# Long convolutions of a hybrid encoder layer: the filters' spectra as one stream of pieces through DRAM, and the second stage on unsplit spectra

## The chip, the cores and the metric

The kernel runs on one core of a Trainium2 chip. A core has five engines that run side by side, each in its own program order: TensorE (PE, matrix products and transposes, with weight loads shown as PEld), VectorE (DVE), ScalarE (ACT), GpSimd (POOL) and SyncE (SP), and 16 DMA engines that serve queues filled by SP, ACT and POOL. They wait for each other through semaphores. The metric is the device time of one execution in microseconds (us); lower is better.

## What is computed

One layer of a bidirectional encoder on 2048 tokens of 1024 channels, in float32. One projection feeds two token mixers, a gated long convolution (Hyena) and an RWKV-7 scan; their outputs are gated, merged and projected, and a SwiGLU feed-forward network follows, each with a layer norm. The change lies in the Hyena branch:

```python
def hyena_filters(L, fw1, ..., fw4, sin_freq):
    ...                                        # a small MLP of the positions, with sines
    h = (h @ fw4).reshape(L, HY_ORDER, 2, HY_WIDTH)
    window = jnp.exp(-t * deltas[None, :])
    return h * window[:, None, None, :]

def long_conv(z, h_fwd, h_bwd, d_skip):        # FFT of length 2L
    zf = jnp.fft.rfft(z, n=n, axis=1)
    hf = jnp.fft.rfft(h_fwd, n=n, axis=0) + jnp.conj(jnp.fft.rfft(h_bwd, n=n, axis=0))
    y = jnp.fft.irfft(zf * hf[None], n=n, axis=1)[:, :L]
    return y + z * d_skip

def hyena_mixer(u, ...):
    v, x1, x2 = jnp.split(short_conv3(u, conv_w, conv_b), 3, axis=-1)
    z = x1 * long_conv(v, h[:, 0, 0], h[:, 0, 1], sk[0])
    z = x2 * long_conv(z, h[:, 1, 0], h[:, 1, 1], sk[1])
    return z
```

There are 512 channels, so 8 filter spectra of 128 channels: 4 channel blocks c by 2 orders o.

## The kernel before

The kernel first projects (with the RWKV preparation woven in), then runs the RWKV scan (`chain`) beside the rest of the projection, then the long convolutions (`hyena`), then merges, and ends with the feed-forward network. On PE the order in `chain` and `hyena` is written out by hand; on the other engines a scheduler orders instructions by priority and readiness. Inside a hand-written order, side work is a generator, and `pull(gen, need)` takes pieces from it until their stated costs reach `need`.

A transform of length 4096 is done in two stages, 128 times 32. For one channel block:

- `fwd` multiplies z with the first-stage matrices (`Fz`, L1220); ACT copies the result to a tile U (L1222), laid out as 128 partitions (4 groups of 32) by 32 by 128 channels.
- `flip` (L1182 to 1188) swaps the two indices of 32 with four DVE transposes (L1187) per tile, each on 32 channels, into a tile V (three buffers).
- `step3` (L1235) multiplies V, four of its 32 slices at a time (q from 0 to 7), with the second-stage matrix `Mc`. For a filter (`load`, L1244) it does so in four f32 matmuls of 128 columns (L1241), and the result H and a copy with the 32-row groups exchanged, Hs, go to ring tiles; the exchange is four DMAs on SP's queue (L1251). For z (`parts`, L1225) each group from q = 1 on is split first into a rounded part and a rest, by a cast on ACT and a subtraction on DVE, and three 128x512 matmuls (L202, 203 and 204, through `mm3`) follow.
- `product` (L1254) runs over q: it loads H for q + 2, transforms z, multiplies by H and by Hs on DVE (A and B, L1278 and L1279), pulls pieces of filter work, and transforms back (L1263, L1264) into a tile Q, which is flipped as well. `inverse` (L1288) is the last stage (L1293); for the first order DVE multiplies the result with x1 into z (L1355), which goes through `fwd` again.

A filter is made by the generator `filt(c, o)` (L1145): for each q, ACT writes the window (four exponentials, L1166), PE multiplies the MLP's output with fw4 (L1167), DVE multiplies the two (L1171), one piece; then `spec` multiplies with the first-stage matrix (L1157), and ACT copies into a tile U (L1158), another piece. After 16 pieces the tile is flipped by `flip`, that is on DVE, and kept in `Vfs`. Both kinds of piece use eight PE instructions. Each filter is a generator of its own: (0, 0) begins in the last two steps of the scan and ends in the prelude of `hyena`, where it is pulled dry; (c, 1) is pulled in the first product of block c and after it, and (c + 1, 0) in the second product of block c.

The blocks c = 0 to 3 follow each other in `hyena` (L1338): transform of filter (c, 0), end of the block before (`finish`: inverse, copies L1310 on ACT, transposes L1302, products with x2), first product, inverse and forward again, the next block's z, second product, the next block's forward.

Scratch for this stage is a ring of 14 tiles (`ring`, L619; `next`, L1096) and tiles `cu` for the rows that the short convolutions (`short`, L1118) fetch from DRAM.

Of the kernel before, what the change touches and what calls it, by code (L numbers as in the profile page):

```python
# [16 lines left out]
P = 128  # L17
# [5 lines left out]
HT = 4  # L23
# [166 lines left out]
class Layer:  # L190
# [38 lines left out]
    def build(self):  # L229
        tc, nc = self.tc, self.nc  # L230
        with tc.tile_pool(name="dr", bufs=1, space=DRAM) as dr, tc.tile_pool(name="keep", bufs=1, reuse_waits="tile") as keep:
# [8 lines left out]
            self.Yd = T("Yd", [NCH, P, 256])  # L240
            self.Nd, self.Wd = T("Nd", [2, P, 1024]), T("Wd", [2, P, 1024])
# [377 lines left out]
    def ring(self, k, n=512):  # L619
        return self.cm.tile([P, 514], F32, name="rg", tag=f"rg{k % 14}")[:, 0:n]  # L620

    def chain(self):
# [3 lines left out]
        with tc.tile_pool(name="ch", bufs=1, reuse_waits="tile") as s, tc.tile_pool(name="chp", bufs=1, space=PSUM, reuse_waits="tile") as ps:  # L626
# [369 lines left out]
            with tc.manual_schedule(engines={mybir.EngineType.PE}):  # L996
# [18 lines left out]
                for n in range(N):  # L1015
# [5 lines left out]
                    if n == LAST + 1:  # L1021
                        taps = self.filt(0, 0)
# [43 lines left out]
    def open(self):  # L1066
# [3 lines left out]
        cu = self.wp.tile([P, 1024], F32, name="cu0", tag="wraw", bufs=2)  # L1070
# [3 lines left out]
        self.turns = dict(cu=0, row=0, w=0, g=0, A=0, B=0, H=0, Hs=0)  # L1074
        self.smalls, self.Vfs = {}, {}
# [20 lines left out]
    def next(self, name):  # L1096
        first, n = dict(w=(8, 2), g=(10, 2), A=(12, 2), B=(0, 2), H=(2, 3), Hs=(5, 3))[name]
# [47 lines left out]
    def filt(self, c, o):  # L1145
        nc = self.nc
        mm = nc.tensor.matmul
        fw4, delta, skip = self.smalls.pop((c, o))
        if (c, o) != (HT - 1, 1):
            self.small(c + o, 1 - o)  # L1150
        U = self.pre(c)

        def spec(q, g):
            ps, tag, bufs = self.fps
            p = ps.tile([P, 4, P], F32, name="pf", tag=tag, bufs=bufs)
            for j in range(4):
                mm(p[:, j], self.Fc[:, 4 * q + j], g[:, j], start=True, stop=True)  # L1157
            nc.scalar.copy(U[:, 4 * q:4 * q + 4], p)  # L1158

        for q in range(8):  # L1160
            win, g = self.next("w"), self.next("g")
            ps, tag, bufs = self.fps
            p = ps.tile([P, 4, P], F32, name="pg", tag=tag, bufs=bufs)
            for j in range(4):
                n = 4 * q + j
                nc.scalar.activation(win[:, j], delta, AF.Exp, scale=self.tcol[:, n:n + 1])  # L1166
                mm(p[:, j], self.H3[:, n], fw4, start=True, stop=n != 0)  # L1167
                if n == 0:
                    mm(p[:, j], self.e0[0:1], skip[0:1], start=False, stop=True)
            with self.tc.high_priority(offset=2 * FIRST):  # L1170
                nc.vector.tensor_tensor(out=g, in0=p, in1=win, op=ALU.mult)  # L1171
# [19 lines left out]
    def hyena(self):  # L1191
# [3 lines left out]
        with tc.tile_pool(name="hy", bufs=1, reuse_waits="tile") as s, tc.tile_pool(name="hyp", bufs=2, space=PSUM, reuse_waits="tile") as ps:  # L1195
# [29 lines left out]
            def parts(V, q, room):  # L1225
                v = V[:, 4 * q:4 * q + 4]
                if q == 0:
                    return v, None
# [452 lines left out]
```

## Time and profile before

| | us |
|---|---|
| median of 3 runs | 4077.75 |
| lowest and highest run | 4075.48 and 4081.51 |
| profiled execution | 4068.93 |
| its span in the profile | 4067.2 |

A profile has one execution. Its page gives the busy time of each engine; other views of the same trace give busy time by stretches of the span, the waits of an engine (who waited, for what, total time, times, longest), groups of instructions by line and tile, the DMA issues, and a timeline in which a bracket holds the idle time before an instruction and what released it. Times in the views are from the span's start. Names such as L1187 are lines of the kernel before; `V<-U` is output and input tile. The stage of the long convolutions is from about 1668 to 2212 us.

### The profile page before, as it was taken

To read this page: it belongs to the slowest core of one execution; us is meant where nothing else is said; L and a number is where in the kernel's file an instruction comes from. 1 tells how busy PE (TensorE), PEld (TensorE's weight loads), DVE (VectorE), ACT (ScalarE), POOL (GpSimd) and SP (SyncE) were. 2 spreads that over 40 slices of the span, in tenths; PEclk is the share of its full clock that TensorE was granted. 3 is DMA by queue.
4 is the path that set the end of the run, shared out by engine and by line. 5 is a ranking of instruction groups with operands and counts; after the bars stand their busy time and mean duration, and the time that the engine had idled before them with its cause. 6 is when DMAs were issued, how large, how long until landed. Compare 5 with 4: busy or idle time off the path is not lost. (4 is left out here: it accounts for less than half of the span.)

```text
span 4067.2 us, 64483 instructions
## 1 busy us (share of the span) xinstructions
PE 3870.1 (95%) x25872; PEld 3130.6 (77%) x25872; DVE 2421.1 (60%) x3823; ACT 1484.1 (36%) x2912; POOL 76.8 (2%) x107
## 2 busy tenths in 40 slices
PE   8999999899998999888898999999999999999998
PEld 6766557677776777788887899788888878888887
DVE  5456885556656666778877656544444465444444
ACT  3345662223335556756554323211111141111113
POOL 0000000000000000000000000000000000000000
PEclk9999999899898999899999999999999999999999
DMA  4556877666666766412224433411111133111111
GB/s 137 175 168 176 224 205 236 192 195 184 201 205 193 205 198 192 118 50 70 63 74 135 159 114 123 160 58 52 47 47 47 47 104 104 47 47 47 47 47 42
DMA packets 389186, 501.83 MB, mean 123 GB/s; under 512 B 134852, under 2 KB 270541, under 8 KB 388181
## 3 DMA queue, kind: packets, MB, share of 16 engines
q1 hardware_dynamic: 362775, 443.13, 36.3%
q10 hardware_dynamic: 20736, 37.80, 3.1%
q0 software_dynamic: 5376, 16.78, 1.5%
q8 instruction: 204, 3.34, 0.3%
q14 instruction: 95, 0.78, 0.1%
HBM read 352.74 MB, written 127.93 MB: 118 GB/s over the span
## 5 line engine op out<-in xcount | busy, mean ns | idle before, releaser
L202 PE MATMUL acc<-xh,wh 128*128 128x512 f32 x1376 | 606.4, 441 | 9.1 <-ACT xh L197 9.1
L203 PE MATMUL acc<-xl,wh 128*128 128x512 f32 x1376 | 551.9, 401 | 6.4 <-DVE xl L198 6.4
L204 PE MATMUL acc<-xh,wl 128*128 128x512 f32 x1376 | 551.0, 400 | 0.5 <-DVE wl L198 0.5
L1618 DVE TENSOR_TENSOR acc<-pd,acc 128x1024 f32<-128x1024 f32 x320 | 387.7, 1221 | 69.9 <-PE pd L204 64.2
L197 ACT CAST fwh<-raw 128x1024 fp32r<-128x1024 f32 x132 | 138.6, 1050 | 704.7 <-PE pg L203 487.9
L202 PEld LDWEIGHTS acc<-xh,wh 128*128 128x128 f32 x1376 | 262.3, 191 | 127.4 <-issue 46.9
L1646 DVE TENSOR_TENSOR h<-pu,sg 128x512 f32<-128x512 f32 x88 | 60.9, 692 | 493.1 <-PE pu L204 485.7
L204 PEld LDWEIGHTS acc<-xh,wl 128*128 128x128 f32 x1376 | 262.8, 191 | 63.9 <-DVE wl L198 1.0
L203 PEld LDWEIGHTS acc<-xl,wh 128*128 128x128 f32 x1376 | 264.5, 192 | 57.4 <-DVE xl L198 10.2
L198 DVE TENSOR_TENSOR wl<-wraw,wh 128x512 fp32r<-128x512 f32 (+1 forms) x217 | 170.3, 792 | 188.4 <-ACT wh L197 181.2
L202 PE MATMUL pd<-fwh,hh 128*128 128x512 f32 x704 | 276.1, 392 | 2.3 <-DVE acc L1616 1.9
L204 PE MATMUL pu<-fxh,fwl 128*128 128x512 f32 x704 | 277.8, 395 | 0.0
L204 PE MATMUL pg<-fxh,fwl 128*128 128x512 f32 x704 | 277.8, 395 | 0.0
L202 PE MATMUL pg<-fxh,fwh 128*128 128x512 f32 x704 | 276.7, 393 | 0.2 <-DVE fxl L1533 0.2
L203 PE MATMUL pg<-fxl,fwh 128*128 128x512 f32 x704 | 276.8, 393 | 0.0
L203 PE MATMUL pu<-fxl,fwh 128*128 128x512 f32 x704 | 276.4, 393 | 0.0
L202 PE MATMUL pu<-fxh,fwh 128*128 128x512 f32 x704 | 275.9, 392 | 0.4 <-ACT fxh L1532 0.4
L203 PE MATMUL pd<-fwl,hh 128*128 128x512 f32 x704 | 275.6, 391 | 0.0
L204 PE MATMUL pd<-fwh,hl 128*128 128x512 f32 x704 | 274.6, 390 | 0.0
L198 DVE TENSOR_TENSOR fwl<-raw,fwh 128x1024 fp32r<-128x1024 f32 x132 | 161.3, 1222 | 166.6 <-ACT fwh L197 162.6
L197 ACT CAST wh<-wraw 128x512 fp32r<-128x512 f32 (+1 forms) x217 | 151.1, 705 | 198.3 <-PE acc L203 182.0
L1187 DVE STREAM_TRANSPOSE V<-U 128x1024 f32<-128x1024 f32 x96 | 181.1, 1955 | 34.3 <-ACT U L1222 14.1
(299 smaller groups left out, 7617.1 us busy)
## 6 DMA issues: line engine op xcount, KB each, us to landing
wraw<-in_w_in SPq DMA_DIRECT2D x130, 512.0 KB
ABp<-ABd SPq DMA_DIRECT2D x64, 512.0 KB
raw<-in_fg SPq DMA_DIRECT2D x44, 512.0 KB
raw<-in_fu SPq DMA_DIRECT2D x44, 512.0 KB
raw<-in_fd SPq DMA_DIRECT2D x44, 512.0 KB
ud<-ev ACTq DMA_DIRECT2D x84, 256.0 KB
ABd<-AB SPq DMA_DIRECT2D x32, 512.0 KB
gated<-ev SPq DMA_DIRECT2D x64, 256.0 KB
```

Of the source, the lines that this page charges most:

```text
L197: nc.scalar.copy(hi, src)
L198: nc.vector.tensor_tensor(out=lo, in0=src, in1=hi.bitcast(F32), op=ALU.subtract)
L202: mm(ps, ah, bh, start=start, stop=False)
L203: mm(ps, ah, bl, start=False, stop=False)
L204: mm(ps, al, bh, start=False, stop=stop)
L1187: self.nc.vector.transpose(V[:, :, sl].rearrange("p j c -> p c j"), U[:, :, sl].rearrange("p n c -> p c n"))
L1618: tt(out=acc[t], in0=pf, in1=acc[t], op=ALU.add)
L1646: tt(out=h, in0=put, in1=sg, op=ALU.mult)
```

## The change

Filters become one generator, `filters`, over all (c, o). A spectrum piece no longer goes into a tile U: ACT copies it to one of two spots (a free half of `cu0`, and ring tile 11) and issues a store of it to a new DRAM tensor `Hd`, with the two indices swapped in the store's address pattern. A filter that is needed is then loaded into V by four DMAs on SP's queue, each to 32 partitions, contiguous in DRAM (`turned_filter`). So the filters use no DVE transpose. The window and its product with the MLP's output share a tile, three in turn instead of two and two. In `product`, z is transformed without the split: step 3 is four f32 matmuls for every q. The next filter is asked for at the end of q = 6. The amounts pulled from the one stream are new.

```diff
+            self.Hd = T("Hd", [HT, 2, 32, P, P])
...
     def ring(self, k, n=512):
-        return self.cm.tile([P, 514], F32, name="rg", tag=f"rg{k % 14}")[:, 0:n]
+        return self.cm.tile([P, 514 if k % 14 == 13 else 512], F32, name="rg", tag=f"rg{k % 14}")[:, 0:n]
...
-                        taps = self.filt(0, 0)
+                        taps = self.filters()
...
-        cu = self.wp.tile([P, 1024], F32, name="cu0", tag="wraw", bufs=2)
+        cu = self.wp.tile([P, 1026], F32, name="cu0", tag="wraw", bufs=2)
...
+        self.spots = [cu[:, 514:1026], self.ring(11)]
...
-        first, n = dict(w=(8, 2), g=(10, 2), A=(12, 2), B=(0, 2), H=(2, 3), Hs=(5, 3))[name]
+        first, n = dict(w=(8, 3), A=(12, 2), B=(0, 2), H=(2, 3), Hs=(5, 3))[name]
...
+    def filters(self):
+        for c in range(HT):
+            for o in range(2):
...
+                def spec(q, g):
+                    ps, tag, bufs = self.fps
+                    p = ps.tile([P, 4, P], F32, name="pf", tag=tag, bufs=bufs)
+                    for j in range(4):
+                        mm(p[:, j], self.Fc[:, 4 * q + j], g[:, j], start=True, stop=True)
+                    u = self.spots[q % 2].rearrange("p (a b) -> p a b", b=P)
+                    nc.scalar.copy(u, p)
+                    nc.scalar.dma_start(self.Hd[c, o, 4 * q:4 * q + 4].rearrange("n p c -> p n c"), u)
...
+                for q in range(8):
+                    g = self.next("w")
...
+                        nc.scalar.activation(g[:, j], delta, AF.Exp, scale=self.tcol[:, n:n + 1])
...
+                        nc.vector.tensor_tensor(out=g, in0=p, in1=g, op=ALU.mult)
...
+                self.made.append((c, o))
...
+    def turned_filter(self, c, o):
+        while (c, o) not in self.made:
+            next(self.taps)
+        V = self.hy.tile([P, 32, P], F32, name="V", tag="post", bufs=3)
+        for k in range(4):
+            self.nc.sync.dma_start(V[32 * k:32 * k + 32], self.Hd[c, o, :, 32 * k:32 * k + 32])
+        return V
...
-            def step3(hi, lo, q):
+            def step3(v, q):
                 p = ps.tile([P, 4, P], F32, name="pz", tag="pz")
-                if lo is not None:
-                    self.mm3(...)
-                    return p
                 for j in range(4):
-                    mm(p[:, j], Mc[:, 0 if 4 * q + j == 0 else 3], hi[:, j], start=True, stop=True)
+                    mm(p[:, j], Mc[:, 0 if 4 * q + j == 0 else 3], v[:, 4 * q + j], start=True, stop=True)
...
-                    p = step3(*zs.pop(q), q)
-                    if q < 7:
-                        zs[q + 1] = parts(Vz, q + 1, room)
+                    p = step3(Vz, q)
...
-                    pull(fill, share if q < 7 else 0.0)
+                    if q < 7:
+                        pull(self.taps, share)
                     if q > 0:
                         back(q - 1)
+                    if q == 6:
+                        Vf = self.turned_filter(*nxt) if nxt else None
...
-                taps, moves = self.taps, turned(self.z0, z)
+                moves = turned(self.z0, z)
                 pull(moves, 0.88)
+                Vf = self.turned_filter(0, 0)
                 U = self.pre(1)
                 for q in range(4):
-                    pull(taps, 3.5)
+                    pull(self.taps, 2.6)
                     pull(moves, 0.44)
                     fwd(z, U, q)
-                pull(taps, 1e9)
...
-                    Q = product(Vf, Vz, self.pre(c + 1), taps, 0.8, "z", hs)
-                    pull(taps, 20.0)
+                    Q, Vf = product(Vf, Vz, self.pre(c + 1), 0.8, hs, (c, 1))
+                    pull(self.taps, 7.8)
...
-                    pull(taps, 1e9)
-                    taps = self.filt(c + 1, 0) if more else iter(())
-                    Vf = self.Vfs.pop((c, 1))
-                    Q = product(Vf, Vz, self.pre(c), taps, 3.0, "x1", {q: load(Vf, q) for q in range(2)})
-                    pull(taps, 1e9)
+                    pull(self.taps, 3.4)
+                    hs = {q: load(Vf, q) for q in range(2)}
+                    Q, Vf = product(Vf, Vz, self.pre(c + 1), 1.6, hs, (c + 1, 0) if more else None)
```

A piece is counted as 0.87 in these amounts, so 2.6 takes three pieces, 0.8 one, 7.8 nine, 3.4 four and 1.6 two. The tiles `vh` and `Ms` of the split, `parts` and `Vfs` go.

79 lines of the change are left out of this document (25 added, 54 removed).

## The prediction

> **What bounds the kernel now.** I read the page's totals, then a view of busy time by stretches over the long-convolution stage, then the waits of TensorE (PE) in it, then the timeline around the longest.
>
> ```profile
> span 4067.2 us, 64483 instructions
> ...
> PE 3870.1 (95%) x25872; PEld 3130.6 (77%) x25872; DVE 2421.1 (60%) x3823; ACT 1484.1 (36%) x2912; POOL 76.8 (2%) x107
> ```
>
> PE is busy 95% of the span, but that is a mean. The change touches one stage, from about 1668 to 2212 us. The next rows are stretches of it, up to the third block's end; columns are PE, weight load, DVE, ACT, POOL busy, then granted clock, DMA share and GB/s.
>
> ```profile
> 1668.00:1760.00 92.00, 79.58 (x613) 73.94 (x612) 77.63 (x86) 53.97 (x109) 0.00 (x0) 0.89 0.25 63
> 1760.00:1894.00 134.00, 118.80 (x1004) 110.68 (x1002) 107.74 (x124) 78.70 (x165) 0.00 (x0) 0.96 0.25 66
> 1894.00:2028.00 134.00, 118.19 (x1007) 110.33 (x1008) 109.14 (x126) 79.44 (x167) 0.00 (x0) 0.97 0.25 66
> 2028.00:2162.00 134.00, 117.53 (x990) 109.94 (x990) 103.59 (x116) 73.28 (x155) 0.00 (x0) 0.95 0.26 73
> ```
>
> The last three rows are one period per channel block each. PE works 118 of 134 us, DVE 107: PE bounds the stage, and 16 us a period are gaps. What ends the gaps over the stage (us, times, longest):
>
> ```profile
> PE pz L1241 <- DVE V L1187: 15.9, 5, 6.0
> PE pfz L1220 <- DVE z L1355: 11.0, 8, 1.5
> PE pv L1302 <- ACT rg L1310: 8.8, 4, 2.9
> PE pg L1167 <- DVE rg L1171: 8.7, 10, 2.2
> PE pz L202 <- DVE rg L1279: 4.9, 3, 1.7
> ```
>
> These five are 49.3 us, nearly all of them DVE. DVE's timeline and PE's show which work is in the way, in the period 1760 to 1894:
>
> ```profile
> 1873.28 1.97 DVE L1187 STREAM_TRANSPOSE V<-U 128x1024 f32<-128x1024 f32 x1 [1.21 <-ACT U L1158]
> 1875.15 1.25 DVE L1355 TENSOR_TENSOR z<-po,x 128x512 f32<-128x512 f32 x2
> 1876.31 5.63 DVE L1187 STREAM_TRANSPOSE V<-U 128x1024 f32<-128x1024 f32 x3
> ```
>
> ```profile
> 1894.34 1.13 PE L1241 MATMUL pz<-V,Mc 128*128 128x128 f32 x8 [3.06 <-DVE V L1187]
> ```
>
> The first and third rows, released by the filter's copy (L1158), are the flip of the next filter: 7.6 us of DVE around the z products that PE is waiting for. In the last row PE waits for the flip of the spectrum itself: it runs out of other work 3.06 us before that ends.
>
> **Part 1: the filter flips leave DVE.** Eight filters times four transposes, 32 x about 1.9 us, are 61 us of DVE. What PE gets back:
> - The z products no longer queue behind them. Of 11.0 us I take 9.5; a product's own delay behind the inverse transform stays.
> - At the period's other end four such transposes stand ahead of the spectrum's own four, in one piece of 14.78 us (so a flip is 7.4):
>
> ```profile
> 1940.15 14.78 DVE L1187 STREAM_TRANSPOSE V<-U 128x1024 f32<-128x1024 f32 x8 [2.90 <-ACT U L1265]
> ...
> 1954.96 1.14 ACT L197 CAST vh<-V 128x512 fp32r<-128x512 f32 x2 [3.78 <-DVE V L1187]
> 1956.01 1.07 ACT L1310 COPY rg<-po 128x512 f32<-128x512 f32 x2
> 1956.64 1.37 PE L1302 MATMUL pv<-k_c_ident,rg 128*128 128x128 f32 x8 [2.86 <-ACT rg L1310]
> ```
>
> ACT stands 3.78 us at the cast of vh, which needs the flip, and the copies L1310 wait behind it in ACT's order; PE waits 2.86 us for them. The change takes away both the four transposes and the cast. I take 8.6 of 8.8 us.
> - L202's wait for L1279 has the same cause (below, the filter's flip just ahead of the A and B products). I take 4.5 of 4.9.
>
> ```profile
> 2056.57 5.69 DVE L1187 STREAM_TRANSPOSE V<-U 128x1024 f32<-128x1024 f32 x3 [1.87 <-ACT U L1158]
> ```
>
> **Part 2: pieces of filters pulled elsewhere.** The pull of 3.4 ahead of the second product puts four pieces (two of the g kind, two of the spectrum kind), 4 x 0.89 = 3.6 us of PE, into the wait of 3.06 us. Of the 15.9 us in five waits the longest, 6.0, is block 3's, and I leave 1.4 to the first one, in the prelude: the three others, -8.5 us, go. The pieces are not extra work, only moved. But the stream is used up before block 3: with 12 pieces pulled in the prelude, the 128 pieces end in the second product of block 2. In block 3 the flip of the first product's result (7.4 us, and an estimated 1.2 for the last copy and its hand-overs) then has nothing beside it, where today filter pieces stand there with about a quarter of the 8.7 us of gaps, 2.2: +6.4 us. The 6.0 us wait for block 3's second spectrum stays. The prelude gets 12 x 0.89 = 10.7 us of pieces that block 3 loses, a wash; its six copies and stores on ACT may stand in PE's way, between 0 and 6 x (0.57 + 0.37, rows below) = 5.6 us, and I take the middle, +3. The wait L1167 for L1171 is the result's own flip interleaved with g products; it stays.
>
> **Part 3: the unsplit spectrum.** For q from 1 to 7 of each of 8 products, a cast, a subtraction and three 128x512 matmuls give way to four f32 matmuls, which the trace shows as eight instructions.
>
> ```profile
> 2050.43 1.06 PE L1241 MATMUL pz<-V,Mc 128*128 128x128 f32 x8
> 2051.24 0.48 PE L202 MATMUL pz<-vh,Ms 128*128 128x512 f32 x1
> 2051.56 0.39 PE L203 MATMUL pz<-vh,Ms 128*128 128x512 f32 x1
> 2051.78 0.40 PE L204 MATMUL pz<-vh,Ms 128*128 128x512 f32 x1
> 2052.02 1.05 PE L1157 MATMUL pf<-rg,Fc 128*128 128x128 f32 x8
> 2052.91 1.06 PE L1167 MATMUL pg<-fw,H3b 128*128 128x128 f32 x8
> ```
>
> Starts give the pace: an f32 group of eight takes 2052.91 - 2052.02 = 0.89 us. The filter group and the three together take 2052.02 - 2050.43 = 1.59 us, where two f32 groups will take 1.78. So +0.19 us, 56 times: **+10.4 us of PE**, on the bounding engine. The group below gives 34 us less ACT (the subtractions about as much less DVE), worth nothing by itself beyond part 1, because PE ends last in the products.
>
> ```profile
> L197 ACT CAST vh<-V 128x512 fp32r<-128x512 f32 x56 | 33.7, 616 | 30.0 <-DVE V L1187 22.9 <-PE pz L204 6.1
> ```
>
> **Part 4: what is added, 64 stores from ACT and 32 loads on SP's queue.** The stores' shape (256 KB in rows of 512 B) is that of the first row (issue ns: least, median, most):
>
> ```profile
> L900 SPq DMA_DIRECT2D yrd<-yo x16: 370/371/650, 1269.7 to 1663.7; - x16
> ```
>
> ```profile
> 432.11 0.72 ACT L505 ACTIVATE spare<-k,k_k_k 128x512 f32<-128x512 f32 x1
> 432.25 0.33 ACTq L345 DMA_DIRECT2D ud<-ev  x1
> ...
> 432.74 0.57 ACT L527 COPY vt<-pp 128x512 f32<-128x512 f32 x1
> ```
>
> In the lower rows a store is issued from ACT's sequencer while the engine runs L505, and L527 starts before L505 has ended: no bubble. So 64 issues cost ACT between 0 and 64 x 0.37 = 24 us; ACT is at 79 of 134 us and loses 34 us of casts, so I take 0 outside the prelude. Behind a store that waits for its copy stand ACT's copies for PE, the exponentials above all.
>
> A filter's four loads move 2.1 MB in rows of 16 KB. The one transfer of that size and row length is the store of H3d; its issue and a stretch just after it:
>
> ```profile
> L303 SPq DMA_DIRECT2D H3d<-H x1: 330/330/330, 147.2 to 147.2; - x1
> ```
>
> ```profile
> 150.00:154.00 4.00, 4.00 (x19) 3.22 (x18) 0.22 (x1) 1.31 (x2) 0.00 (x0) 1.00 0.88 364
> ```
>
> At 364 GB/s a filter takes 5.8 us, and some 2.2 more to land (of the 3.6 us of a 0.5 MB row quoted below, 1.4 are transfer): 8.0. The tightest user is the next block's first filter: asked for after q = 6 of the second product, needed after step 3 of q = 7 (0.89), two returns and four forward steps (sixteen instructions each, 6 x 1.78): 11.6 us later. Cost 0. Without that cover it would be some 8 us, three times. The Hs exchanges of the same product are issued ahead of the loads; behind them on SP stand the next product's exchanges, which need the loads anyway, and the short convolutions' row fetches, whose user is a transpose several microseconds on. The merged win and g tile and the ring's new sizes change no instruction: 0.
>
> The Trainium skill (SBUF — State Buffer, "Door 1: The DMA port swizzle") says that a transfer on 32 partitions reaches half the ports, with 189 GB/s for 1 MiB. No run here shows such a load; by that page the estimate is 11.1 us plus the landing, 1.7 over the cover, three times, and the sum would be 5 us higher.
>
> **The clock.** The four rows of stretches lose 10.1 + 5.4 + 4.0 + 6.7 = 26 us to a clock under 1.00. The dips lie in the stretches with gaps. Bounds: nothing comes back, or about 20. With some half of the gaps gone, but new ones in block 3, I take -6, nearer the lower end.
>
> The Trainium skill (TensorE: Matmul & The Clock Gate, "What's actually happening") has the clock halve after an idle window of about 3.4 us. The gaps here that go are each under 3.1 us, so by that rule they gave no dip and -6 would be 0, the sum 6 us higher. The trace has dips in periods with no longer gap (0.96 and 0.97), which speaks against its strict form.
>
> **The sum**: waits -9.5 - 8.6 - 4.5 - 8.5 = -31.1; block 3 +6.4; prelude +3; unsplit matmuls +10.4; clock -6: **-17.3 us**. The profiled execution took 4068.9 us (its span and 1.7 around it), 8.8 under the median of the runs, 4077.75. I carry the difference to the median: **4060 us**.
>
> **Rivals.**
> - *PE is the bound and other waits take over* (slower). Each removed DVE wait may be followed by another late arrival at the same place: flips of the result and the spectrum remain. For it: PE at 118 of 134 us. Against: the rows name a filter transpose or a cast directly ahead of each wait. If none of the 31.1 us comes, and no clock, +10.4 + 6.4 + 3 = +19.8: 4098. It is slower from where less than 11 of the 31.1 come. Chance 0.10.
> - *The stores' round trip holds ACT.* Two spots: a copy waits until the store two spectra earlier has landed, and ACT's other work stands behind it. Landing times are shown only for GpSimd's queue:
>
> ```profile
> Nd<-G POOLq DMA_DIRECT2D x32, 128.0 KB, 6.0
> ...
> Wd<-W POOLq DMA_DIRECT2D x8, 512.0 KB, 3.6
> ```
>
> At 3.6 us a spectrum may come every (0.57 + 0.37 + 3.6) / 2 = 2.3 us, which hides beside the result's flip (a transpose of 1.9 and a product of 0.6, 2.5 us). At 6.0 it is 3.5 us: three pulls of 4.5 spectra x 1.0 and a prelude of 6 x 1.7 (against 1.78 of PE) make +24, about 4084. For it: those loads share the engines. Against: DMA share is 0.25. Chance 0.10.
> - *The loads are late*: each writes a quarter of the partitions, and at half the row's rate they take 11.5 + 2.2 us, 2.1 over the cover, three times: 4066, chance 0.08. *The clock gives nothing*: 4066, chance 0.06.
> - The forecast, 4042 to 4069, takes the rest, 0.66.
>
> **Range and chances.** A measurement of this kernel tells about 0.2% (8 us) from no change. Forecast and the last two rivals are faster; a little of them, and most of the store rival, lies within 0.2%. Faster 0.79, same 0.11, slower 0.10. For 8 in 10 the range runs from 4040 (all clock back) to 4078, leaving out the PE rival and much of the store rival.
>
> **What would show it.** After: transposes x64; no vh; L1241-type groups in step 3 at 0.89; pfz waiting for z under 3 us in all; pv's wait gone; pz's wait for V near 8 (block 3 and the start); a new po wait for V of 8 to 9 in block 3; periods near 125 us. Wrong if spots' copies wait for a DMA, if pz waits for a DMA into V, or if the periods stay at 134 us.

## The result, and the profile after

| | before | after |
|---|---|---|
| median | 4079.63 us (4 runs) | 4107.94 us (4103.86 to 4113.11, 4 runs) |
| ratio | | 1.0067, 95% interval 1.0046 to 1.0088 |
| profiled execution, span | 4068.93, 4067.2 | 4106.86, 4105.1 |

The change makes the kernel slower; the forecast was 4060. Two later comparisons of the same kernel on other chips gave 1.0107 (1.0089 to 1.0126) and 1.0105 (1.0083 to 1.0128): after's median was 4107 and 4105 there, before's 4065 and 4066. So the loss is 28 to 41 us.

The totals of after's page, to be held against the prediction's first fence:

```profile
span 4105.1 us, 65058 instructions
...
PE 3882.2 (95%) x26152; PEld 3147.7 (77%) x26152; DVE 2331.8 (57%) x3734; ACT 1454.7 (35%) x2855; POOL 76.8 (2%) x107
```

DVE lost 89 us and ACT 29, as meant, and PE gained 12; the time still rose. The reading that sorts it out is one stretch, from the last scan step on PE to the merge's first matmul with the Hyena weights, `pm<-y,whh` ("the stage" from here on). First before's row of it, then after's: the stretch, its length, busy time and count of PE, weight load, DVE, ACT, POOL, then granted clock, DMA share and GB/s.

```profile
1649.40:2212.30 562.90, 493.84 (x4115) 460.39 (x4114) 440.46 (x512) 322.89 (x682) 0.00 (x0) 0.95 0.26 69
```

```profile
1657.00:2257.70 600.70, 510.34 (x4396) 483.75 (x4394) 350.58 (x424) 295.74 (x627) 0.00 (x0) 0.93 0.46 120
```

The stage is 37.8 us longer: PE is busy 16.5 us more, and idle 21.3 us more (69.1 against 90.4). The rest of the span differs by +7.6 ahead of the stage and -7.5 behind it; another profile of after has the stage's start at 1649.7, so the +7.6 lies within what executions of one kernel vary by. Three profiles of after have the stage at 600.7, 601.0 and 599.1 us, so a stage compares kernels within some 2 us where the granted clock is alike.

By stretches, the prelude (up to the first inverse) grew from 87.3 to 110.0 us, 10.7 of it busy time and 12.0 idle time of PE; from there to block 3 the time rose from 336.4 to 348.6, nearly all of it busy time (+11.0); block 3, up to the last inverse, rose from 124.9 to 127.8.

What ended PE's gaps in after's stage (us, times, longest):

```profile
PE pv L1303 <- ACT rg L1311: 12.8, 4, 7.4
PE pz L1243 <- ACT rg L1249: 10.7, 6, 3.3
PE po L1294 <- DVE V L1203: 7.9, 1, 7.9
PE ph L1222 <- DVE cu L1129: 7.7, 1, 7.7
PE pv L1303 <- DVE co L1305: 6.4, 3, 3.3
PE pz L1243 <- DVE V L1203: 5.3, 1, 5.3
...
PE ph L1222 <- ACT x L1225: 3.7, 2, 3.4
```

The z products' wait (11.0) and the wait for L1279 (4.9) are gone, and pz's wait for V fell from 15.9 to 5.3. In their place pv waits 19.2 us (8.8 before), ph, the transposes of the short convolutions' rows, waits over 11 us where before it had almost none, and pz waits 10.7 us for ACT's copies L1249. The timeline shows one chain behind the first two. (pz's three longest waits, 2.5 to 3.3 us, end behind exponentials, an exchange of H and a convolution in ACT's order; no version of the changed kernel below takes them away.) At the boundary of blocks 0 and 1 in after (start, duration, engine, operation; in brackets the idle time before it and what released it):

```profile
1823.71 1.55 SPq L1194 DMA_DIRECT2D V<-Hd  x3
...
1825.30 1.07 SPq L1132 DMA_DIRECT2D cu<-ud  x2
...
1834.66 14.75 DVE L1203 STREAM_TRANSPOSE V<-U 128x1024 f32<-128x1024 f32 x8 [2.90 <-ACT U L1266]
...
1841.65 1.52 ACT L1134 ACTIVATE cv<-cu,k_conv_b,k_conv_w 128x512 f32<-128x512 f32 x2
...
1850.05 1.08 DVE L1140 SCALAR_TENSOR_TENSOR co<-cu,k_conv_w,cv 128x512 f32<-128x512 f32 x1
...
1851.16 0.33 SPq L1132 DMA_DIRECT2D cu<-ud  x1
...
1854.27 0.81 ACT L1134 ACTIVATE cv<-cu,k_conv_b,k_conv_w 128x512 f32<-128x512 f32 x1 [8.63 <-DMA cu<-ud]
1854.99 0.56 ACT L1311 COPY rg<-po 128x512 f32<-128x512 f32 x1
...
1855.61 1.12 PE L1303 MATMUL pv<-k_c_ident,rg 128*128 128x128 f32 x4 [7.37 <-ACT rg L1311]
```

Read it upward from the last row. PE waits for the copy L1311. The product that it copies (`po`, L1294) had ended at 1846.6, but the copy stands behind the convolution's third batch in ACT's order; ACT stands 8.63 us there for a row; the row's fetch waits for one of two row buffers; the buffer is freed by DVE's L1140, and that stands behind the flip of 14.75 us. The first two rows come late as well: the buffers' last user had ended at 1797.9, but on SP the fetches stand behind the exchanges of H and the next filter's loads. Before, the same convolution was over by then: its rows were fetched and used inside the second product.

```profile
1771.80 1.07 SPq L1130 DMA_DIRECT2D cu<-ud  x2
...
1776.28 0.82 ACT L1132 ACTIVATE cv<-cu,k_conv_b,k_conv_w 128x512 f32<-128x512 f32 x1
...
1785.12 0.81 ACT L1132 ACTIVATE cv<-cu,k_conv_b,k_conv_w 128x512 f32<-128x512 f32 x1 [0.90 <-DMA cu<-ud]
```

The Trainium skill (PSUM — Partial Sum Buffer, "Engine vs sequencer instructions") calls the queues of ScalarE and VectorE strict FIFO. The rows agree: a copy of 0.56 us, needed by PE, left some 8 us late behind an instruction it had nothing to do with.

### The profile page after: what moved, and what is told of

Same layout as the page of the kernel before. It is cut to its first block, busy times and chain, and to the rows that moved or that the text cites. A ratio compares the mean times of both kernels' runs of the same rounds, so it can differ in the third digit from the quotient of the medians.

```text
span 4105.1 us, 65058 instructions
## 1 busy us (share of the span) xinstructions
PE 3882.2 (95%) x26152; PEld 3147.7 (77%) x26152; DVE 2331.8 (57%) x3734; ACT 1454.7 (35%) x2855; POOL 76.8 (2%) x107
## 4 chain that ended last, share of the span: by engine, by line
PE 45%; DVE 3%; DMA 1%; ACT 1%; issue 0%; SPq 0%; ACTq 0%; DVEq 0%
PE pg L202 4%; PE pg L204 4%; PE pu L203 4%; PE pu L202 4%; PE pg L203 4%; PE pu L204 4%; PE pd L202 4%; PE pd L204 4%; PE pd L203 4%; PE pm L204 1%; PE pm L202 1%; PE pm L203 1%; PE po L203 1%; PE po L202 1%; PE po L204 1%; PE pz L1243 1%
## 5 line engine op out<-in xcount | busy, mean ns | idle before, releaser
L202 PE MATMUL acc<-xh,wh 128*128 128x512 f32 x1376 | 606.2, 441 | 11.5 <-ACT xh L197 11.5
L204 PE MATMUL acc<-xh,wl 128*128 128x512 f32 x1376 | 550.9, 400 | 0.5 <-DVE wl L198 0.5
L1611 DVE TENSOR_TENSOR acc<-pd,acc 128x1024 f32<-128x1024 f32 x320 | 387.8, 1222 | 69.9 <-PE pd L204 64.3
L202 PEld LDWEIGHTS acc<-xh,wh 128*128 128x128 f32 x1376 | 262.3, 191 | 131.0 <-issue 47.4
L204 PEld LDWEIGHTS acc<-xh,wl 128*128 128x128 f32 x1376 | 262.7, 191 | 64.3 <-DVE wl L198 1.0
L198 DVE TENSOR_TENSOR wl<-wraw,wh 128x512 fp32r<-128x512 f32 (+1 forms) x217 | 170.5, 793 | 193.0 <-ACT wh L197 184.8
L202 PE MATMUL pd<-fwh,hh 128*128 128x512 f32 x704 | 276.7, 393 | 1.8 <-DVE acc L1609 1.4
L202 PE MATMUL pu<-fxh,fwh 128*128 128x512 f32 x704 | 276.3, 393 | 0.5 <-ACT fxh L1525 0.5
L202 PE MATMUL pg<-fxh,fwh 128*128 128x512 f32 x704 | 276.5, 393 | 0.2 <-DVE fxl L1526 0.2
L204 PE MATMUL pg<-fxh,fwl 128*128 128x512 f32 x704 | 276.4, 393 | 0.0
L204 PE MATMUL pu<-fxh,fwl 128*128 128x512 f32 x704 | 276.1, 392 | 0.0
L204 PE MATMUL pd<-fwh,hl 128*128 128x512 f32 x704 | 274.8, 390 | 0.0
L198 DVE TENSOR_TENSOR fwl<-raw,fwh 128x1024 fp32r<-128x1024 f32 x132 | 161.4, 1222 | 166.6 <-ACT fwh L197 162.7
L202 PEld LDWEIGHTS pd<-fwh,hh 128*128 128x128 f32 x704 | 132.0, 188 | 40.1 <-DVE acc L1611 6.6
```

What stands on the lines that cost most here:

```text
L198: nc.vector.tensor_tensor(out=lo, in0=src, in1=hi.bitcast(F32), op=ALU.subtract)
L202: mm(ps, ah, bh, start=start, stop=False)
L204: mm(ps, al, bh, start=False, stop=stop)
L1611: tt(out=acc[t], in0=pf, in1=acc[t], op=ALU.add)
```

## The experiments

All are timed with their own runs of before. The stage's numbers come from each kernel's profile: length = PE busy + idle, and PE's mean granted clock.

| kernel | stage | PE busy | idle | clock | ratio (95% interval) |
|---|---|---|---|---|---|
| before | 562.9 | 493.8 | 69.1 | 0.95 | |
| after | 600.7 | 510.3 | 90.4 | 0.93 | 1.0067 (1.0046-1.0088) |
| a_again (after) | 601.0 | 512.1 | 88.9 | 0.92 | 1.0107 (1.0089-1.0126) |
| a_third (after) | 599.1 | 509.4 | 89.7 | 0.93 | 1.0105 (1.0083-1.0128) |
| b_unsplit | 575.9 | 506.0 | 69.9 | 0.95 | 1.0037 (1.0020-1.0053) |
| b_turned | 601.7 | 499.4 | 102.3 | 0.91 | 1.0118 (1.0086-1.0151) |
| b_pool_cast | 565.7 | 492.2 | 73.4 | 0.95 | 1.0004 (0.9989-1.0019) |
| a_split | 605.7 | 501.2 | 104.5 | 0.91 | 1.0115 (1.0090-1.0140) |
| a_rows_pool | 601.6 | 505.6 | 96.0 | 0.92 | 1.0115 (1.0090-1.0140) |
| a_loads_pool | 630.3 | 509.8 | 120.5 | 0.91 | 1.0193 (1.0172-1.0215) |
| a_short_early | 594.0 | 508.1 | 85.9 | 0.93 | 1.0104 (1.0089-1.0119) |
| a_short_early_split | 603.5 | 502.9 | 100.6 | 0.92 | 1.0119 (1.0102-1.0137) |
| a_blocks_early | 585.7 | 503.8 | 82.0 | 0.94 | 1.0067 (1.0043-1.0091) |
| a_three_rows | 580.3 | 502.0 | 78.3 | 0.94 | 1.0074 (1.0050-1.0098) |
| a_lean | 577.4 | 502.2 | 75.2 | 0.94 | 1.0030 (1.0014-1.0047) |
| a_all | 608.1 | 512.9 | 95.2 | 0.90 | 1.0139 (1.0111-1.0166) |
| a_lean_rows | 584.7 | 509.0 | 75.7 | 0.93 | 1.0085 (1.0067-1.0104) |
| a_lean_early | 593.3 | 515.7 | 77.6 | 0.92 | 1.0064 (1.0043-1.0085) |
| a_lean_rows_early | 580.1 | 503.9 | 76.2 | 0.95 | 1.0088 (1.0063-1.0113) |
| a_lean_split_pool | 582.1 | 494.0 | 88.1 | 0.93 | 1.0083 (1.0056-1.0110) |

### The change in its two halves

b_unsplit: before, with step 3 as in after (four f32 matmuls for every q, no cast, no subtraction).

```diff
-                    p = step3(*zs.pop(q), q)
-                    if q < 7:
-                        zs[q + 1] = parts(Vz, q + 1, room)
+                    p = step3(Vz, q)
...
```

> The kernel before with only the second stage on unsplit spectra. By PE's pace +10.4 us of work, less the waits that the casts cause (8.8 us at the transposes of finish, if my reading of that row is right): 4075 to 4085. If the 8.8 us wait was for the flip and not for the cast, +10: 4088 to 4092.

```profile
1652.40:2228.30 575.90, 506.00 (x4396) 479.20 (x4395) 407.66 (x456) 291.40 (x626) 0.00 (x0) 0.95 0.25 67
```

PE busy rose by 12.2 us, the idle time not at all (69.9 against 69.1), and the ratio is 1.0037, about 15 us. Unsplit products cost what they add to PE; my 10.4 was small. The run also answers the question on the cast: there is none left, and pv still waits, for DVE now.

```profile
PE pv L1285 <- DVE co L1287: 7.7, 5, 2.3
```

b_turned: before, with each filter stored from U and loaded into V by four DMAs at the end of its generator, in before's order.

```diff
+            nc.scalar.dma_start(self.Hd[c, o, 4 * q:4 * q + 4].rearrange("n p c -> p n c"), U[:, 4 * q:4 * q + 4])
...
-        self.Vfs[c, o] = self.flip(U)
+        V = self.hy.tile([P, 32, P], F32, name="V", tag="post", bufs=3)
+        for k in range(4):
+            nc.sync.dma_start(V[32 * k:32 * k + 32], self.Hd[c, o, :, 32 * k:32 * k + 32])
+        self.Vfs[c, o] = V
```

> The kernel before with only the filters' flip taken from DVE to DRAM (stores from ACT out of the old tile, four loads on SP where the transposes stood), the old generators and amounts. If DVE's flips of the filters are what PE waits for (the prediction's first step), 15 to 20 us faster: 4060 to 4065. Theory Q: the loads wait on SP in program order and hold what stands behind them: no gain or slower, 4075 to 4100.

```profile
PE pz L1246 <- DMA V<-Hd: 23.3, 5, 9.5
PE pz L1246 <- ACT rg L1252: 21.8, 4, 8.1
PE pq L1269 <- DVE rg L1284: 21.5, 3, 7.5
```

57 us of DVE left the stage, and PE's idle time rose by 33 us. With no lead, PE waits for the load itself (23.3 us), and SP stands 19.4 us ahead of the loads for the stores to land; the wait for L1284 is for exchanges of H, for which DVE waits 23.1 us. At 4113 the kernel is slower than either expectation allowed.

a_split: after with the split put back.

```diff
-                    p = step3(Vz, q)
+                    p = step3(*zs.pop(q), q)
+                    if q < 7:
+                        zs[q + 1] = parts(Vz, q + 1, room)
...
```

> The changed kernel with the split of the spectrum put back (cast, subtraction, three matmuls), all else kept. Theory W: PE gets 10.4 us back, 4095 to 4100. Theory Q: the casts are more work in ACT's order, so part of the 10.4 is lost again: 4098 to 4110. If the split were in fact the cheaper form by more than PE's pace says, under 4094.

No gain: PE is busy 9 us less and idle 14 us more than in after. The largest PE waits are pv for ACT's copies, 20.0 us, and ph for cu, 19.8; and ACT itself waits at the cast:

```profile
ACT vh L197 <- DVE V L1203: 34.9, 8, 7.5
```

Before had 22.9 us in this row. So taking PE's added work out of the changed kernel by way of the split buys nothing: there PE waits.

### Queues

a_rows_pool: after with the convolutions' row fetches on GpSimd's queue. a_loads_pool: after with the loads of V there.

```diff
-            nc.sync.dma_start(u[:, lo:hi], self.ud[...])
+            nc.gpsimd.dma_start(u[:, lo:hi], self.ud[...])
```

```diff
-            self.nc.sync.dma_start(V[32 * k:32 * k + 32], self.Hd[...])
+            self.nc.gpsimd.dma_start(V[32 * k:32 * k + 32], self.Hd[...])
```

> The changed kernel with only the row fetches of the short convolutions moved from SP's queue to GpSimd's. Theory Q (SP's in-order queue: the filter loads, and what waits ahead of them, delay the row fetches; ACT then stands at the short convolution's activation and PE at the transposes of finish): the waits of pv for L1311 (12.8 us), of ph for the row tile and for x (13 us) and most of pz for L1249 (10.7 us) go, 20 to 30 us in all, near 4080. Theory W (the bound is PE's added work, 10.4 us, and the uncovered flips of block 3; fetches late only by accident): less than 8 us come back, over 4098. Theory D (the fetch waits for DVE to release its row tile, behind 14.8 us of flips, whichever queue it is on): the pv wait stays at 3 us or more a block, 4088 to 4098.

> The kernel after with the 32 loads of turned filters on GpSimd's queue. Theory A2, the loads stand on SP ahead of the row fetches and wait there for their stores: the fetches leave earlier and 10 to 20 us come back (ratio 0.003 to 0.005 under the unchanged copy). Theory A, the fetches wait for DVE to free their two buffers, not for the loads: under 0.001 of change, and cv still waits some 30 us for cu<-ud.

Neither is faster; the second is clearly slower (1.0193 against 1.0107 on the same chip), a load's median landing there being 8.6 us (6.7 on SP's queue, from the five landings that after's trace has) and pz waiting 29.4 us for L1249. At the boundary shown above SP's order did matter: with the fetches on GpSimd's queue the same convolution runs at 1803 to 1816, ahead of the flip, and pv's wait for the copies falls from 12.8 us in the stage to this:

```profile
PE pv L1303 <- ACT rg L1311: 1.9, 2, 1.8
```

But SP's queue is not all of it. a_rows_pool has two longer waits, 14.5 and 14.8 us, and the second, in the prelude, shows the same chain with SP taken out of it:

```profile
1711.71 7.33 DVE L1203 STREAM_TRANSPOSE V<-U 128x1024 f32<-128x1024 f32 x4
...
1720.23 1.98 DVE L1140 SCALAR_TENSOR_TENSOR co<-cu,k_conv_w,cv 128x512 f32<-128x512 f32 x2
1721.83 0.55 POOL L1132 DMA_DIRECT2D cu<-ud  x1 [9.10 <-DVE co L1140]
...
1725.25 0.82 ACT L1134 ACTIVATE cv<-cu,k_conv_b,k_conv_w 128x512 f32<-128x512 f32 x1 [8.81 <-DMA cu<-ud]
...
1728.73 1.97 PE L1222 MATMUL ph<-k_c_ident,co 128*128 128x128 f32 x8 [14.81 <-ACT x L1225]
```

Here the fetch waits for DVE's L1140, behind the flip, on GpSimd's queue too.

### When the short convolutions come

a_again is after unchanged, the reference on that chip. a_short_early asks for each convolution about one product earlier; a_short_early_split also puts the split back; a_blocks_early leaves the prelude as in after. The lines are those of a_blocks_early; the other two have one more, in the prelude.

```diff
                     pull(moves, 1e9)
+                    more = c + 1 < HT
+                    zo = self.short(c + 1, True) if more else None
+                    x2 = self.short(2 * HT + c, False)
                     Q, Vf = product(Vf, Vz, self.pre(c + 1), 0.8, hs, (c, 1))
...
-                        pull(turned(self.short(c + 1, True), z), 1e9)
-                    x2 = self.short(2 * HT + c, False)
+                        pull(turned(zo, z), 1e9)
+                        xo = self.short(HT + c + 1, True)
```

> The kernel after, unchanged, on the same chip as the three that follow. From the two results so far (1.0067, interval 1.0046 to 1.0088, on the first chip): a ratio of 1.005 to 1.009. If it reads 1.011 or more here, the earlier runs with row fetches on GpSimd's queue and with the split spectrum (both 1.0115) were no slower than after, and only the chip differed.

> The kernel after with each short convolution (row fetch, one ACT and two DVE operations, four batches) asked for about one product earlier; TensorE's order and all work unchanged. Theory A, the convolutions come too late: after's trace has TensorE waiting 12.8 us for L1311 behind cv, 7.7 for cu, 6.4 for co, 3.7 for x and part of 10.7 for L1249, some 35 us that stood at next to nothing before; most goes, the ratio falls by 0.005 to 0.009 under the unchanged copy, to about 0.999, and ACT's waits of cv for cu<-ud (31.9 us) fall under 10. Theory B, the loss is TensorE's added work and the round trip through DRAM: within 0.002 of the unchanged copy, and the waits come back under other names.

> The early convolutions and the split of the second spectrum put back. If the unsplit products cost what they cost alone on before (14 us, 1.0037), this is 0.002 to 0.0035 under the early convolutions alone, about 0.996, and beats both kernels. If ACT's casts and DVE's subtractions bring the filter work into a wait again, as the split alone on after did, it is no faster than the early convolutions alone.

> After with the convolutions asked for one product earlier in the blocks only; the prelude as in after. The kernel with all of them early took 6.5 and 4.2 us less than after in the stretches that end at the first inverse of blocks 1 and 2, and 3.1 and 5.6 less in block 3, but lost 8 in the prelude. Theory A: these gains stay, 15 to 20 us without the prelude's loss, ratio 0.004 to 0.005 under after's (1.0107 on one chip, 1.0067 on another). Rival: the loss in the prelude was the price of the gains (the same waits moved), and nothing is left: within 0.001.

In the blocks the waits fell (pv for L1311 from 12.8 to 2.2 us), but with the prelude's convolution moved as well, one wait of 12.3 us for x came there, and the total did not move. Without that move the stage is 15 us shorter than after's (585.7), and the median some 11 us lower (4094.6 against 4105 to 4108), less than the 15 to 20 I expected. The timing alone doesn't show that gain: the ratio, 1.0067, was taken on another chip, and after's own three range from 1.0067 to 1.0107. The split again gained nothing on top of a_short_early.

a_three_rows: after with a third row buffer, at the price of one g tile.

```diff
+            self.cus.append(self.ring(10, 514))
...
-            u = self.cus[self.turns["cu"] % 2]
+            u = self.cus[self.turns["cu"] % len(self.cus)]
...
-        first, n = dict(w=(8, 3), ...
+        first, n = dict(w=(8, 2), ...
```

> After with a third buffer for the short convolutions' rows (taken from the g tiles, three to two). Theory A3: with two buffers a convolution's later batches are fetched only when DVE has freed a buffer, DVE stands in the 7.3 us flip at that point, and ACT holds TensorE's copies behind the convolution that waits for the row. With three, one batch more is there before the flip: ACT's waits of cv for cu<-ud (30 us in after) fall by a third or more, TensorE's waits for L1311, x and cu (24 us) by 8 to 15, the ratio by 0.002 to 0.004 under after's. Rival: the order in which ACT meets the convolutions sets it, not the buffers: within 0.001 of after.

ACT's waits at cv in after, then in a_three_rows:

```profile
ACT cv L1134 <- DMA cu<-ud: 31.9, 12, 8.6
```

```profile
ACT cv L1134 <- DVE co L1140: 3.5, 4, 1.6
...
ACT cv L1134 <- DMA rg<-ud: 3.2, 2, 2.5
```

With them went pv's wait for the copies (12.8 to 2.5) and ph's waits for cu and x (11.4 to 0.5). So the chain behind these two is shown, though not that the buffer alone broke it: with three buffers the scheduler also placed the convolutions earlier, and block 1's rows are used at 1764 to 1787, long before the flip. pz's wait for the copies of H did not go:

```profile
PE pz L1244 <- ACT rg L1250: 11.4, 6, 6.9
```

The price of the chain in time is less sure: the stage is 20 us shorter, but that profile is of the fastest of five runs (4084.5 against a median of 4102.3), and the ratio's interval overlaps those of after's copies.

### Where the pieces stand

a_lean: pieces just in time.

```diff
-                        pull(self.taps, share)
+                        pull(self.taps, share if share > 0.5 or q % 2 else 0)
...
-                    pull(self.taps, 2.6)
+                    pull(self.taps, 0.8)
...
-                    Q, Vf = product(Vf, Vz, self.pre(c + 1), 0.8, hs, (c, 1))
+                    Q, Vf = product(Vf, Vz, self.pre(c + 1), 1.6, hs, (c, 1))
...
-                    Q, Vf = product(Vf, Vz, self.pre(c + 1), 1.6, hs, (c + 1, 0) if more else None)
+                    Q, Vf = product(Vf, Vz, self.pre(c + 1), 0.4, hs, (c + 1, 0) if more else None)
```

> After with the stream of pieces made just in time: one piece instead of three beside each forward group of the prelude, two instead of one per step of the first product, one every other step instead of two of the second. Eight pieces (7.1 us) leave the prelude, and 14 to 16 come into block 3's first product, which has none in after. Theory C: the pieces pulled ahead cost the prelude their full time and give block 3 little back, since its wait for the flip stays: the stretch to block 3's first inverse keeps within 4 us of its 64.3, the periods before it fall, and the total falls by 7 to 14 us. Rival (the prediction's wash): pieces cost the same wherever they stand, within 3 us.

The best version of the changed kernel: 1.0030, 4080.8 us (10 runs). The stage in stretches, first after, then a_lean: the prelude to the first inverse, then to block 3's forward transform, then block 3.

```profile
1657.00:1767.00 110.00, 86.97 (x708) 82.19 (x706) 53.92 (x72) 65.23 (x155) 0.00 (x0) 0.91 0.51 131
1767.00:2115.60 348.60, 309.50 (x2715) 294.59 (x2714) 207.13 (x251) 182.17 (x386) 0.00 (x0) 0.95 0.48 124
2115.60:2243.40 127.80, 101.32 (x851) 96.02 (x850) 79.86 (x87) 41.29 (x72) 0.00 (x0) 0.89 0.35 94
```

```profile
1658.60:1758.10 99.50, 84.50 (x697) 80.20 (x696) 60.86 (x84) 67.81 (x157) 0.00 (x0) 0.91 0.59 151
1758.10:2085.20 327.10, 292.83 (x2593) 277.57 (x2592) 200.50 (x240) 169.28 (x357) 0.00 (x0) 0.96 0.48 123
2085.20:2217.70 132.50, 109.88 (x982) 105.21 (x980) 81.13 (x86) 52.10 (x98) 0.00 (x0) 0.92 0.42 109
```

Block 3 took in 16 pieces (851 to 982 PE instructions, about 14.2 us at 0.89) and grew by 4.7 us only: there they fill gaps. The prelude has nearly the same work (708 and 697 instructions) and is 10.5 us shorter, since both row buffers were free before the flip began, and the waits for cu and x are gone. So part of a_lean's gain is the chain of the rows again. The later pieces have a price: pz waits 7.6 us for filters' loads (3 times, up to 4.7), a wait that after does not have.

a_all joins three rows, early blocks, lean pieces and the split. a_third is after again; a_lean_rows, a_lean_early and a_lean_rows_early are combinations without the split ("early" in the blocks only), and their edits are those above.

> All of it together: three row buffers, convolutions early in the blocks, pieces just in time, and the second spectrum split again; of the change only the way of the filters through DRAM is left. If theories A and C hold and the unsplit products cost their 10 to 14 us, some 45 us come off after: 4060, at or under before. If it stays above 1.003, the way through DRAM costs by itself what the local flips cost.

> After, unchanged, beside the three combinations on one chip: a ratio of 1.006 to 1.011, as in its two earlier comparisons.

> Pieces just in time and three row buffers. Alone they took 24 and 21 us off the stage (577 and 580 us from the last scan step to the merge, 601 in after). If they remove different waits (PE work too early in one, rows behind the flip in the other), together 35 to 45: the stage at 556 to 566, ratio about 1.000. If both only relieve the same stand of ACT in the prelude, no more than the better one: 575, ratio 1.003.

> Pieces just in time and convolutions early in the blocks (alone 15 us off the stage). If different waits: stage 562 to 568, ratio about 1.001; if the same: 575 to 577, ratio 1.003.

> All three with the unsplit spectrum; the kernel with the split had ACT standing 46 us at the cast of vh for the flip. If that stand is what made it slow, this is 35 us or more under it: ratio at or under 1.003. If the three collide by themselves, it stays above 1.008 and ACT stands elsewhere.

The gains do not add: no combination is better than a_lean alone, and a_lean_rows and a_lean_early come out above both of their expectations. The idle times are 75.2, 75.7, 77.6 and 76.2 us, as if the edits relieved the same stand and what one has taken were not there for the next; that is a reading, since the lists of waits behind these sums differ. The remaining spread in the stage is PE's busy time for the same instructions, 502 to 516 us, which goes with the clock (0.92 to 0.95). a_all, which I had expected at or under before, is 1.0139: ACT stands 45.9 us at the cast of vh for the flip (8 times, up to 7.9), and PE idles 95.2 us. Without the split it is 22 us faster (a_lean_rows_early, on another chip, 4102.6 against 4125.0), less than the 35 that I had set for the cast's stand as the only reason.

### The cast taken off ACT

b_pool_cast: before with the casts of vh on GpSimd. a_lean_split_pool: a_lean with the split, casts on GpSimd.

```diff
-                    self.split(hi, lo, v)
+                    nc.gpsimd.tensor_copy(hi, v)
+                    nc.vector.tensor_tensor(out=lo, in0=v, in1=hi.bitcast(F32), op=ALU.subtract)
```

> Before with the 56 casts of vh on GpSimd instead of ACT; all else as before. My prediction put TensorE's wait for L1310 (8.8 us) and L1279 down to ACT standing at the cast for the flip. Theory S: the cast's stand is the cause, the wait for L1310 falls from 8.8 to under 3 us and the stage (562.9) to about 550; ratio 0.997 to 0.999. Rival: the flip itself is what TensorE would wait for, and the wait comes back at the second product's first steps: within 0.001 of before. A cast on GpSimd is not in any trace here; if it takes over 2 us, each of the products' 28 steps behind the first may wait for it and the kernel is slower.

> Pieces just in time, the split spectrum with its casts on GpSimd: no local filter flips, no stand of ACT at the flip, no added TensorE work. If the unsplit products' cost is their 12 us of TensorE (before with them alone: busy 493.8 to 506.0, idle the same 69 to 70), the stage falls from the 577 of pieces just in time to 560 to 567, ratio 0.998 to 1.001. If the casts on GpSimd are too slow for the steps, it is above 1.005.

b_pool_cast, no change in time, is the test of a step of the prediction. The boundary of blocks 1 and 2, where the prediction showed ACT standing at the cast:

```profile
1940.46 14.78 DVE L1187 STREAM_TRANSPOSE V<-U 128x1024 f32<-128x1024 f32 x8 [2.84 <-ACT U L1266]
...
1950.03 0.59 ACT L1311 COPY rg<-po 128x512 f32<-128x512 f32 x1 [0.45 <-PE po L1294]
...
1955.10 1.13 DVE L1305 TENSOR_TENSOR co<-pv,co 128x512 f32<-128x512 f32 x1
...
1956.38 0.63 PE L1303 MATMUL pv<-k_c_ident,rg 128*128 128x128 f32 x4 [2.30 <-DVE co L1305]
```

ACT's copy now comes at 1950, on time, and PE waits as before, for the product L1305 on DVE, behind the same eight transposes. Over the stage pv waits 12.6 us for it (8.8 for ACT before). The cast was in the way, but the flip was behind it, as in b_unsplit.

a_lean_split_pool, at 1.0083 against an expected 1.001 at most: PE is busy 8 us less than in a_lean, and idle 13 us more; pv waits 17.1 us for DVE. Again work taken from PE comes back as waiting.

## Why the prediction was wrong

Rival one, "PE is the bound and other waits take over", is nearest to what happened; it had a chance of 0.10 and a price of 4098. Its mechanism, that the flips of the result and the spectrum remain, holds for pv. The longer new waits, for the rows of the short convolutions, it does not name. By the prediction's own steps:

| step | predicted | shown |
|---|---|---|
| z products' wait | -9.5 | -11.0 |
| waits ahead of the second product, block 3's flip | -8.5, +6.4 | pz for V -10.6, po for V +5.3 |
| L202's wait for L1279 | -4.5 | -4.9 |
| pv's wait | -8.6 | +10.4 |
| rows of the short convolutions (ph) | 0 | +13.3 |
| copies of H (pz for L1249) | 0 | +9.0 |
| unsplit products | +10.4 | +12.2 (b_unsplit) |
| stores, loads | 0 | no wait of pz for a load; on SP the loads stand ahead of the row fetches |
| clock | -6 | about +4 in PE's busy time |
| prelude's idle time | +3 | +12.0: ph's waits (above) and the pieces' copies |
| the moved pieces | "a wash" | busy +10.7 in the prelude, -12.1 in block 3's first half |

The rows of waits are after's minus before's in the stage: ph goes from 1.6 to 14.9 us (all releasers), pz for L1249 from 1.7 (with L202's) to 10.7. What is left of the idle time's +21.3 is some 10 us in other rows, the longest 4.7 (`pr` L204 for L198). A period, from one block's forward transform to the next, was to be near 125 us; it went from 134 to 141.

**The step that failed first is "The change takes away both the four transposes and the cast. I take 8.6 of 8.8 us."** I took four of the eight transposes in the 14.78 us row for the filter's. They are the flip of the second product's result and the flip of the spectrum, and neither leaves: after has the same row (14.75 us, x8). The row itself said so, its releaser being L1265, the copy of the product's result; a filter's flip is released by L1158. And b_unsplit and b_pool_cast show that without the cast on ACT the wait stays (7.7 and 12.6 us). That step was worth 0.

**The step that cost most is in part 4: the row fetches' "user is a transpose several microseconds on".** The first user is ACT's cv, in ACT's one order, ahead of copies that PE needs; behind it DVE frees the buffer. I looked at what stands behind the new transfers on SP, and not at what stands behind their user on ACT. a_three_rows takes ACT's stand and both waits away; another queue for the fetches takes pv's away, but not the prelude's. That accounts for ph's +13.3 and for pv's +10.4 (pv waits 9.5 in all in a_three_rows, near before's 8.8). pz's +9.0 for the copies of H stays in a_three_rows and is not explained by the rows.

**"A wash"** holds for the work. First the prelude before (after's row stands with a_lean's above), then block 3's first half, from its first forward matmul to the next inverse, before and after:

```profile
1649.40:1736.70 87.30, 76.31 (x574) 71.21 (x573) 69.37 (x91) 61.72 (x140) 0.00 (x0) 0.86 0.28 73
...
2073.10:2139.10 66.00, 60.15 (x512) 55.85 (x511) 51.41 (x56) 37.27 (x77) 0.00 (x0) 0.97 0.24 69
```

```profile
2115.60:2178.00 62.40, 48.10 (x417) 45.09 (x416) 43.75 (x44) 21.35 (x37) 0.00 (x0) 0.91 0.43 115
```

PE is busy 10.7 us more in the prelude, which is 12 pieces at 0.89, and 12.1 less in block 3's first half. That half is 3.6 us shorter, near the -10.7 + 6.4 that the prediction gave it. What failed is the **+3 for the prelude**: PE's idle time there rose by 12.0 us. Of its waits 11.1 us are for the rows again (ph's 7.7 and 3.4), and 6.9 end on the copies of the pieces (L1163), for which the +3 stood; in exchange some of before's waits are gone. Block 3's second half grew by 6.4 us at a clock of 0.87 (0.94 before).

**Right**: z's wait, the pulls ahead of the second product, block 3's new wait of 8 (7.9), and the transfers. The loads of V in after (count, issue in ns, first and last start; then the landing):

```profile
L1194 SPq DMA_DIRECT2D V<-Hd x32: 302/425/1384, 1684.1 to 2165.5; - x32
...
DMA to landing us min/median/max: 5.0/6.7/7.4
```

I had 8.0 for a filter of four loads; the trace has the landings of five loads; a store landed in 2.7 (median), no pz waited for a DMA in after, and the spots held ACT for 4.2 us in all. By the estimate that the prediction took from the Trainium skill (SBUF — State Buffer, "Door 1: The DMA port swizzle") such loads would have come 1.7 us late; no wait of PE in after shows it. The sign of the unsplit step was right, its size 1.8 us small.

**The clock** went the other way: 0.95 to 0.93 over the stage. The new gaps are longer, and the rows at the end show the clock at half behind the longest; that they make the whole difference is not shown.

What stays open: why a_lean_rows is timed slower than a_lean with the same idle time (they ran on different chips; of the 13.6 us between the two profiled executions 7.3 lie in the stage, with the clock, and 8.7 already ahead of it), what holds the copies of H that pz waits for, and what in the changed kernel turns PE work taken out into waiting even with the cast on GpSimd. No version found beats before; the nearest is a_lean at 1.0030.

## What to carry to other kernels

When work leaves a busy engine, read the releaser of each row before you credit it: it tells whose work the row is, and here 8.6 of the 31.1 us of waits were booked on transposes that stay. When an in-order engine gets new waits or a new order, follow each load to its first user, and list what PE needs that stands behind that user; two small buffers freed by an engine in a long operation are enough to make ScalarE and TensorE wait with it. Side work moved ahead of need costs its time where the engine is full, and is nearly free in a stretch that waits for a latency, as block 3 of a_lean shows: 14.2 us of work for 4.7 us of time.

## What the runs showed of the hardware

A long gap of PE can be paid a second time in the clock. First before, behind a gap of 3.06 us at 1894.34, then after, behind the gaps of 7.7 us (ph for cu) that ends at 1712.64 and of 7.37 at 1855.61 (columns as above):

```profile
1896.00:1900.00 4.00, 4.00 (x22) 3.97 (x22) 2.48 (x5) 1.28 (x4) 0.00 (x0) 0.58 0.29 70
```

```profile
1712.00:1716.00 4.00, 1.97 (x8) 1.57 (x8) 2.44 (x4) 0.00 (x0) 0.00 (x0) 0.50 0.44 113
...
1856.00:1860.00 4.00, 1.84 (x8) 1.04 (x6) 4.00 (x5) 1.28 (x2) 0.00 (x0) 0.50 0.44 104
```

The clock fell to about half for some microseconds each time. The Trainium skill (TensorE: Matmul & The Clock Gate, "What's actually happening") puts the fall behind an idle window of about 3.4 us; here it also followed the gap of 3.06. The gap's length alone does not decide it: in after, behind a gap of 3.07 us that ends at 1940.00, the clock stayed at 1.00.

```profile
1940.00:1944.00 4.00, 4.00 (x35) 4.00 (x36) 2.15 (x4) 1.76 (x5) 0.00 (x0) 1.00 0.34 89
```

A cast of 128x512 on GpSimd took 0.71 us in b_pool_cast (56 of them), little more than ACT's 0.62.
